# Hybrid decoder layer: first weight slice on ScalarE's queue in four pieces, its first cast and the bias table pinned in program order

## The chip, the cores and the metric

The kernel runs on one core of a Trainium2 chip. The metric is device time in microseconds (us), from the start of the program on the chip to its end; lower is better. The time before is the median of three runs.

## The reference

One layer of a hybrid decoder, one inference step over a prompt of 2048 rows and a sample batch of 8 rows, with D_MODEL = 1024:

```python
h = rmsnorm(x, g_norm)
proj = h @ w_in_l                       # 1024 x D_IN
(qa, ka, va, ga, ub, vb, gb, qc, kc, vc, gc, lr) = jnp.split(proj, offs, axis=-1)
ya = swa_prompt(qa, ka, va, rel_bias, sink_l)     # window 128, 8 heads of 64, 2 key heads
yb, v_rows = chunk_mlp(ub, vb, sw_l, sb_l, ln_g_l, ln_b_l)
oc, S_fin = gla(qc, kc, vc, log_a, s0)            # log_a from lr
...
y = jnp.concatenate([ya * jax.nn.silu(ga), yb * jax.nn.silu(gb), yc * jax.nn.silu(gc)], axis=-1)
x = x + (y @ w_out_l).astype(x.dtype)
```

Three mixers share one input projection: A is sliding-window attention with a learned sink for each head and a relative position bias taken from a table of 32 buckets, B a gated MLP over chunks of 128 rows, C a gated linear attention. An output projection and a final RMSNorm follow. Everything is float32.

## The kernel before, in words

**Tiling.** The prompt is cut into 16 x tiles of 128 rows (t = 0 to 15), and two of them make a chunk of 256 rows (c = 0 to 7). A float32 matmul is done as three float16 matmuls: each operand is split into a high and a low half, and PASSES (high by high, high by low, low by high) are summed in PSUM. The projection weights come in slices of columns: A1 holds the keys, the values and the low-rank gate (272 columns), A0 the queries (512), A2 the gate of A (512); the slices of B and C follow much later.

**An x tile.** `x_load` (L240) loads it from SyncE's queue into one of four buffers (`x_bufs`, named sl_1_105 for tiles 0, 1, 4, 5, ... and sl_2_106 for tiles 2, 3, 6, 7, ...). `h_tile` calls `norm_split`: ScalarE squares the tile with a running sum (L244), DVE works out the scale in a chain of small steps (L246, L124 to L134), ScalarE casts the scaled tile to the high half (L248), DVE takes the low half (L249). Then SyncE issues two DMA transposes (L258), one for each half, into a chunk buffer hb. TensorE needs these transposed tiles.

**A weight slice.** `prep_slice` returns five steps. `load` issues DMAs (L164) into float32 staging; for A1, which has two groups of columns, these are eight DMAs in before. `sq` squares it in four steps on ScalarE (L179). `sq2` sums the four columns over the partitions with one small matmul (L185) which is pinned by `tc.keep_in_program_order`, and DVE makes a scale from it (L187 to L192). `split(0, 4)` and `split(4, 8)` do eight casts on ScalarE (L203) and eight low halves on DVE (L204), one for each block of 128 rows of the slice.

**The units.** `unit_va` multiplies a tile by 144 columns of A1 (24 matmuls, L307) and is evicted by L456, L457 and L459; `unit_k` multiplies a chunk by the keys (24 matmuls, L296; evicted by L435 to L438); `unit_q`, four to a chunk, by the queries (L296; L476 on ScalarE, L477 on DVE); `unit_gate`, two to a chunk, by A2 (L307, 512 columns; L486 on ScalarE, L487 on DVE). TensorE works in the order: both tiles' `unit_va`, `unit_k` and four `unit_q` of the first chunk, the same of the second, their four gates, and then chunk by chunk.

**The bias table.** `lc_load` loads its inputs. `lc_bias` multiplies a one-hot table by the bias (L384), DVE copies the result (L386), SyncE writes it to DRAM (L387) and reads it back in two parts with overlapping windows (L391) into two buffers Lp. `lc_bm(0)` and `lc_bm(1)` reverse the rows with two float32 matmuls each (L398), which DVE scales into the table BM (L400). The first scores need BM.

**Attention of a tile.** For each tile and key head: `a_scores` (eight matmuls L506; DVE adds the bias and takes the maximum, L510), `a_soft` (L520 to L527), `a_exp` (L538, four exponentials), `a_split` (cast L548, low half on GpSimd L549, two DMA transposes L563), `a_pv` (L578, L583, L585), and the store of y (L588) after the second key head.

**What sets the order.** The program is traced once; `at(t, f)` puts a function on a list with a time, and `tick` counts the columns of the projection matmuls emitted so far as a clock and calls each function when its time has come. So the units' matmuls set the pace and the other work is traced between them. A scheduler then orders each engine's instructions by their dependences and its own costs; an instruction handed to `tc.keep_in_program_order` stays behind the one traced just before it on its engine. Each engine and each engine's DMA queue then runs strictly in its order. Before the first unit's matmuls, the code at L1300 to L1326 traces in order: `x_load(0)`, the small constants, `x_load(1)`, A1's load, a first part of A0's load, `h_tile(0)`, A1's `sq` and `sq2`, `h_tile(1)`, A1's two `split`s, the rest of A0's load, `x_load(2)`, `x_load(3)`, A2's load, the table's inputs, and A0's `sq`, `sq2` and `split`s. In the list stand `h_tile(2)` at 1, `lc_bias` at 2, `h_tile(3)` at 3, `lc_bm` at 7 and 9, A2's `sq` at 11, its `sq2` and first `split` at 14, its second `split` at 18.

Of the kernel before, what the change touches and what calls it, by code (L numbers as in the profile page):

```python
# [15 lines left out]
AF = mybir.ActivationFunctionType  # L16
# [17 lines left out]
OFF = {}  # L34
# [9 lines left out]
def hybrid_step_kernel(ctx: ExitStack, tc: tile.TileContext, I, O):  # L44
    nc = tc.nc
# [103 lines left out]

    def prep_slice(name, idx, cols, stage, dst, nload=1):  # L150
        n = sum(w for _, w in cols)
# [4 lines left out]
        def load_part(a, b):  # L156
            if "sg" not in st:
                st["sg"] = stage()
            for ap, k0, k1 in st["sg"]:
                lo, hi = max(a, k0), min(b, k1)  # L160
                c = 0
                for off, w in cols:
                    if lo < hi:
                        SP.dma_start(out=ap[:, lo - k0:hi - k0, c:c + w],  # L164
                                     in_=w_in[lo * 128:hi * 128, off:off + w].rearrange("(k p) n -> p k n", p=128))
                    c += w

        def load():
            for a in range(0, 8, 2):
                load_part(a, a + 2)  # L170

# [23 lines left out]
        def split(a, b):  # L195
            def f():
                for ap, k0, k1 in st["sg"]:
                    for k in range(max(a, k0), min(b, k1)):
# [3 lines left out]
                        gk = st["gs"][:, k:k + 1]  # L202
                        S.activation(out=hi, in_=src, func=AF.Copy, scale=gk)  # L203
                        V.scalar_tensor_tensor(out=lo, in0=src, scalar=gk, in1=hi, op0=ALU.mult, op1=ALU.subtract)  # L204
# [162 lines left out]
    lc = {}  # L367
# [26 lines left out]
    def lc_bm(half):  # L394
        def f():
            for q in range(2):
                ps = mbank()
                PE.matmul(ps, lc["fl"], lc[half][:, 2 * q:2 * q + 2, :].rearrange("p a b -> p (a b)"),  # L398
                          start=True, stop=True)
                V.tensor_scalar(out=BM["t"][:, half * 4 + 2 * q:half * 4 + 2 * q + 2, :].rearrange("p a b -> p (a b)"),  # L400
# [897 lines left out]

    if True:
        prA1 = prep_slice("A1", 0, [(OFF["ka"], 256), (OFF["lr"], 16)], stage_h(272), dst_one(272))  # L1300
        prA0 = prep_slice("A0", 1, [(OFF["qa"], 512)], stage_h(512), dst_slot(512))
        prA2 = prep_slice("A2", 2, [(OFF["ga"], 512)], stage_h(512), dst_slot(512))
        x_load(0)
        startup_consts()
        x_load(1)
        prA1[0]()
        LOADP["A0"][0]()
# [50 lines left out]
        at(3.0, lambda: h_tile(3))  # L1358
        at(7.0, lc_bm(0))
        at(9.0, lc_bm(1))  # L1360
        for t in range(4, NTILE):
# [163 lines left out]
```

## Time and profile before

| | before |
|---|---|
| median of three runs | 1192.56 us (1190.77 to 1195.80) |
| the profiled execution, its own time | 1196.03 us |
| its span in the trace | 1194.3 us |
| mean granted clock of TensorE | 0.99 |
| TensorE matmuls (PE) | 1136.0 us, 95% of the span |
| VectorE (DVE) | 677.2 us, 57% |
| ScalarE (ACT) | 480.9 us, 40% |
| GpSimd (POOL) | 72.9 us, 6% |

The times are device time of whole executions; the span is what the trace holds of the profiled one. PE is TensorE's matmuls, PEld its weight loads (which run beside matmuls), SPq a DMA's issue on SyncE. A busy share is an average over the whole span: what a stretch is worth is read from its waits and its timeline. In a row of a timeline the bracket gives how long the engine had been idle, and which instruction or DMA released it. [...]

### The profile page before, as it was taken

How to read it: one execution, taken by the hardware profiler on the slowest of the kernel's cores; microseconds unless marked ns; L12 is line 12 of the kernel's file. 1: busy time of each engine (PE TensorE's matmuls, PEld its weight loads, DVE VectorE, ACT ScalarE, POOL GpSimd, SP SyncE). 2: the span in 40 equal slices, each digit the busy share in tenths (PEclk: the TensorE clock that was granted, in tenths of full speed). 3: DMA queues.
4: the chain of work that ended last, by engine and by line, in shares of the span. 5: the costliest groups of instructions: out<-in, count | busy, mean ns of one | idle time of the engine just before them, and what ended most of it. 6: DMA issues, size and time to landing. Idle time of an engine off the chain costs nothing.

```text
span 1194.3 us, 19595 instructions
## 1 busy us (share of the span) xinstructions
PE 1136.0 (95%) x7637; PEld 663.4 (56%) x7637; DVE 677.2 (57%) x2229; ACT 480.9 (40%) x967; POOL 72.9 (6%) x49
## 2 busy tenths in 40 slices
PE   4997899997998999999999999999999999999997
PEld 3756577775654544444465567566665543444443
DVE  5887866657686355576284355645545643544442
ACT  7776755565771021552265411412212131322220
POOL 0012222222210000000000000000000000000000
PEclk9998999998999999999999999999999999999999
DMA  9579954534454002000054521220114446766641
GB/s 274 158 129 199 190 150 89 75 78 104 112 138 116 18 22 85 8 18 18 18 186 121 207 55 31 94 89 18 54 44 129 121 124 159 208 160 164 165 124 54
DMA packets 196913, 128.63 MB, mean 108 GB/s; under 512 B 155922, under 2 KB 170395, under 8 KB 196819
## 3 DMA queue, kind: packets, MB, share of 16 engines
q1 hardware_dynamic: 196818, 127.36, 41.4%
q8 instruction: 60, 0.98, 0.3%
q14 instruction: 35, 0.28, 0.1%
HBM read 66.36 MB, written 23.63 MB: 75 GB/s over the span
## 4 chain that ended last, share of the span: by engine, by line
PE 59%; DVE 3%; DMA 3%; ACT 2%; issue 1%; SPq 1%; POOL 0%; DVEq 0%; ACTq 0%
PE pp L307 31%; PE pp L1008 14%; PE pp L296 6%; DMA hb<-sl 2%; PE mx L671 1%; PE mx L867 1%; PE mx L849 1%; PE mx L873 1%; PE mx L881 1%; PE mx L320 1%; DMA sl<-y_d 1%; ACT sl L977 1%; SPq L989 1%; DVE sl L997 1%; DMA sl<-in_w_in_dram 0%
## 5 line engine op out<-in xcount | busy, mean ns | idle before, releaser
L307 PE MATMUL pp<-sl,hb 128*128 128x512 f16 x2304 | 516.9, 380 | 1.3 <-DVE qk L477 1.3
L307 PEld LDWEIGHTS <-hb 128*128 128x128 f16 x2688 | 250.2, 99 | 268.8 <-issue 12.5
L1008 PE MATMUL pp<-hb,hb 128*128 128x512 f16 x1152 | 251.2, 380 | 2.5 <-DMA hb<-sl 2.5
L1008 PEld LDWEIGHTS <-hb 128*128 128x128 f16 x1152 | 111.7, 98 | 140.3 <-DMA hb<-sl 5.4
L296 PE MATMUL pp<-hb,sl 128*128 128x256 f16 x1536 | 178.8, 275 | 8.7 <-DVE yy L487 8.6
L296 PEld LDWEIGHTS <-sl 128*128 128x128 f16 x1536 | 149.3, 98 | 31.9 <-issue 11.5
L549 POOL TENSOR_TENSOR phb<-Lp,pha 128x1024 f16<-128x1024 f32 (+1 forms) x32 | 66.5, 2079 | 288.0 <-ACT pha L548 270.9
L1011 DVE SCALAR_TENSOR_TENSOR sl<-pp,finv,sl 128x512 f32<-128x512 f32 x32 | 23.9, 748 | 85.8 <-PE pp L1008 85.8
L486 ACT ACTIVATE yy<-pp,scal 128x512 f32<-128x512 f32 x48 | 32.5, 679 | 81.5 <-PE pp L307 65.4
L994 ACT ACTIVATE sl<-sl 128x1024 f32<-128x1024 f32 (+1 forms) x16 | 16.9, 1056 | 116.8 <-DVE sl L1011 114.8
L538 ACT ACTIVATE Lp<-Lp,sm 128x256 f32<-128x256 f32 (+1 forms) x128 | 62.3, 488 | 0.2
L510 DVE CUSTOM_DVE_ANT_0 Lp<-mx,BM,scal 128x256 f32<-128x256 f32 (+1 forms) x128 | 54.7, 472 | 4.0 <-PE mx L506 3.4
L487 DVE SCALAR_TENSOR_TENSOR yy<-yy,pp 128x512 f32<-128x512 f32 x48 | 32.8, 682 | 42.2 <-ACT yy L486 42.2
L623 ACT ACTIVATE kk<-pp,invs 128x512 f32<-128x512 f32 x16 | 10.9, 683 | 93.3 <-PE pp L307 93.3
L477 DVE SCALAR_TENSOR_TENSOR qk<-pp,qk 64x256 f16<-64x256 f32 x64 | 26.9, 422 | 37.6 <-ACT qk L476 36.8
L978 DVE SCALAR_TENSOR_TENSOR sl<-sl,ch 128x1536 f16<-128x1536 f32 (+1 forms) x17 | 30.9, 1817 | 20.3 <-ACT sl L977 20.3
L977 ACT ACTIVATE sl<-sl,ch 128x1536 f16<-128x1536 f32 (+1 forms) x17 | 26.8, 1575 | 32.1 <-DVE ch L144 32.1
L637 DVE BATCH_NORM_STATS2 sm<-kk 128x6 f32<-128x512 f32 x16 | 11.1, 691 | 50.2 <-ACT kk L623 50.2
L204 DVE SCALAR_TENSOR_TENSOR sl<-sl,gs,sl 128x512 f16<-128x512 f32 x48 | 36.1, 813 | 3.6 <-ACT sl L203 3.3
L506 PE MATMUL mx<-kk,qk 128*128 128x256 f16 (+1 forms) x256 | 33.4, 271 | 4.7 <-DVE sm L510 4.7
L307 PE MATMUL pp<-s,hb 128*128 128x144 f16 x384 | 31.9, 246 | 5.9 <-DMA hb<-sl 3.6
L548 ACT CAST pha<-Lp 128x1024 f16<-128x1024 f32 (+1 forms) x32 | 32.4, 1012 | 5.1 <-DMA pt<-pha 4.7
(320 smaller groups left out, 1234.1 us busy)
## 6 DMA issues: line engine op xcount, KB each, us to landing
sl<-in_x_prompt_dram SPq DMA_DIRECT2D x32, 512.0 KB
sl<-in_w_in_dram SPq DMA_DIRECT2D x24, 512.0 KB
sl<-in_w_out_dram SPq DMA_DIRECT2D x6, 2048.0 KB
sl<-y_d SPq DMA_DIRECT2D x16, 768.0 KB
y_d<-yy SPq DMA_DIRECT2D x32, 256.0 KB
out_dram<-sl SPq DMA_DIRECT2D x15, 512.0 KB
hb<-in_w_in_dram SPq DMA_DIRECT2D x8, 512.0 KB
y_d<-Lp SPq DMA_DIRECT2D x8, 512.0 KB
```

What stands on the lines that cost most here:

```text
L204: V.scalar_tensor_tensor(out=lo, in0=src, scalar=gk, in1=hi, op0=ALU.mult, op1=ALU.subtract)
L296: PE.matmul(ps[:m, :CT], w[:, wl, k, c0:c0 + m], h[:, hl, k, :], start=(n == 0), stop=(n == 23))
L307: PE.matmul(ps[:, :n_], h[:, hl, k, j * 128:(j + 1) * 128], w[:, wl, k, c0:c0 + n_], start=(n == 0), stop=(n == 23))
L486: S.activation(out=g, in_=ps, func=AF.Tanh, scale=hg)
L487: V.scalar_tensor_tensor(out=g, in0=g, scalar=1.0, in1=ps, op0=ALU.add, op1=ALU.mult)
L506: PE.matmul(pv[:, hh, :], Qt[c][:, h // 2, h % 2, j * 128:(j + 1) * 128], Kt[c][:, 2 * hb + hl, ko:ko + W], start=(hl == 0), stop=(hl == 1))
L510: V.tensor_tensor_reduce(out=L[:, i, :], in0=pv[:, hh, :], in1=BM["t"][:, 4 * hb + i, 256 - W:256], scale=cS, scalar=-3e38, op0=ALU.add, o ...
L538: S.activation(out=L[:, i, :], in_=L[:, i, :], func=AF.Exp, bias=nb[:, i:i + 1], accum_out=den[:, i:i + 1])
L548: S.copy(P[0], L)
L549: G.tensor_tensor(out=P[1], in0=L, in1=P[0], op=ALU.subtract)
L977: S.activation(out=d["h"][:, 0, :], in_=d["y"], func=AF.Copy, scale=s)
L1008: PE.matmul(ps, d["yT"][:, hl, k, :], wo[k // 2][:, wl, k % 2, cs], start=(n == 0), stop=(n == 35))
```

## The change

Four things are edited.

- A1's load goes from SyncE's queue to ScalarE's, in two steps of four blocks in place of four steps of two. With A1's two groups of columns that makes four DMAs in place of eight; the bytes are the same. It is also traced ahead of the small constants and of `x_load(1)`.
- The first of A1's eight casts (k = 0) is pinned behind the ScalarE instruction traced just before it, which is x tile 1's cast in `h_tile(1)`.
- The four table matmuls (L398) are pinned in program order on TensorE.
- `lc_bm(0)` and `lc_bm(1)` are called at 12 and 14 in place of 7 and 9.

```diff
--- before.py
+++ after.py
@@ -147,7 +147,7 @@
     LOADP = {}
     INVI = {}
 
-    def prep_slice(name, idx, cols, stage, dst, nload=1):
+    def prep_slice(name, idx, cols, stage, dst, que=nc.sync, step=2):
         n = sum(w for _, w in cols)
         inv = invs[:, idx:idx + 1]
         INVI[name] = inv
@@ -161,13 +161,13 @@
                 c = 0
                 for off, w in cols:
                     if lo < hi:
-                        SP.dma_start(out=ap[:, lo - k0:hi - k0, c:c + w],
-                                     in_=w_in[lo * 128:hi * 128, off:off + w].rearrange("(k p) n -> p k n", p=128))
+                        que.dma_start(out=ap[:, lo - k0:hi - k0, c:c + w],
+                                      in_=w_in[lo * 128:hi * 128, off:off + w].rearrange("(k p) n -> p k n", p=128))
                     c += w
 
         def load():
-            for a in range(0, 8, 2):
-                load_part(a, a + 2)
+            for a in range(0, 8, step):
+                load_part(a, a + step)
 
         def sq():
             st["dst"] = dst()
@@ -200,7 +200,9 @@
                         hi = st["dst"][:, 0, k, :]
                         lo = st["dst"][:, 1, k, :]
                         gk = st["gs"][:, k:k + 1]
-                        S.activation(out=hi, in_=src, func=AF.Copy, scale=gk)
+                        cast = S.activation(out=hi, in_=src, func=AF.Copy, scale=gk)
+                        if name == "A1" and k == 0:
+                            tc.keep_in_program_order(cast)
                         V.scalar_tensor_tensor(out=lo, in0=src, scalar=gk, in1=hi, op0=ALU.mult, op1=ALU.subtract)
             return f
 
@@ -395,8 +397,8 @@
         def f():
             for q in range(2):
                 ps = mbank()
-                PE.matmul(ps, lc["fl"], lc[half][:, 2 * q:2 * q + 2, :].rearrange("p a b -> p (a b)"),
-                          start=True, stop=True)
+                tc.keep_in_program_order(PE.matmul(ps, lc["fl"], lc[half][:, 2 * q:2 * q + 2, :].rearrange("p a b -> p (a b)"),
+                                                   start=True, stop=True))
                 V.tensor_scalar(out=BM["t"][:, half * 4 + 2 * q:half * 4 + 2 * q + 2, :].rearrange("p a b -> p (a b)"),
                                 in0=ps, scalar1=rS, scalar2=-3e38, op0=ALU.mult, op1=ALU.max)
         return f
@@ -1297,13 +1299,14 @@
         return out
 
     if True:
-        prA1 = prep_slice("A1", 0, [(OFF["ka"], 256), (OFF["lr"], 16)], stage_h(272), dst_one(272))
+        prA1 = prep_slice("A1", 0, [(OFF["ka"], 256), (OFF["lr"], 16)], stage_h(272), dst_one(272),
+                          que=nc.scalar, step=4)
         prA0 = prep_slice("A0", 1, [(OFF["qa"], 512)], stage_h(512), dst_slot(512))
         prA2 = prep_slice("A2", 2, [(OFF["ga"], 512)], stage_h(512), dst_slot(512))
         x_load(0)
+        prA1[0]()
         startup_consts()
         x_load(1)
-        prA1[0]()
         LOADP["A0"][0]()
         h_tile(0)
         prA1[1]()
@@ -1356,8 +1359,8 @@
         at(1.0, lambda: h_tile(2))
         at(2.0, lc_bias)
         at(3.0, lambda: h_tile(3))
-        at(7.0, lc_bm(0))
-        at(9.0, lc_bm(1))
+        at(12.0, lc_bm(0))
+        at(14.0, lc_bm(1))
         for t in range(4, NTILE):
             at(HT0 + HTD * (t - 4) - HTL, lambda t=t: x_load(t))
             at(HT0 + HTD * (t - 4), lambda t=t: h_tile(t))
```

The change moves instructions on several queues. Lines of the changed kernel are 2 higher than before from L206 on, and 3 higher from L1304 on; buffer numbers differ.

**ScalarE at the start.** hb_126 and hb_127 (before) or hb_108 and hb_109 (after) are the two halves of A1's staging; sl_105 is x tile 0 and then 1; ch_140 and ch_174 (ch_136 and ch_170) are the scales of x tile 0 and 1; hb_136 (hb_132, hb_133) is A0's staging. Before:

```order
L244 ACTIVATE sl_105,ch_140<-sl_105 128x1024
L179 ACTIVATE s_14_156,sm_157<-hb_126 128x544
L248 ACTIVATE sl_105<-sl_105,ch_140 128x1024
L179 ACTIVATE s_14_156,sm_157<-hb_126 128x544
L179 ACTIVATE s_14_156,sm_157<-hb_127 128x544 x2
L244 ACTIVATE sl_105,ch_174<-sl_105 128x1024
L203 ACTIVATE s_14_156<-hb_126,gs_172 128x272 x4
L203 ACTIVATE s_14_156<-hb_127,gs_172 128x272 x4
L248 ACTIVATE sl_105<-sl_105,ch_174 128x1024
L179 ACTIVATE sl_227,sm_228<-hb_136 128x1024 x2
```

After, where four DMA issues of A1 (L164) also stand ahead of these rows:

```order
L246 ACTIVATE sl_105,ch_136<-sl_105 128x1024
L179 ACTIVATE s_14_152,sm_153<-hb_108 128x544 x2
L179 ACTIVATE s_14_152,sm_153<-hb_109 128x544
L250 ACTIVATE sl_105<-sl_105,ch_136 128x1024
L179 ACTIVATE s_14_152,sm_153<-hb_109 128x544
L179 ACTIVATE sl_223,sm_224<-hb_132 128x1024
L246 ACTIVATE sl_105,ch_170<-sl_105 128x1024
L203 ACTIVATE s_14_152<-hb_108,gs_168 128x272 x3
L203 ACTIVATE s_14_152<-hb_109,gs_168 128x272 x4
L179 ACTIVATE sl_223,sm_224<-hb_132 128x1024
L250 ACTIVATE sl_105<-sl_105,ch_170 128x1024
L203 ACTIVATE s_14_152<-hb_108,gs_168 128x272
```

The cast that is pinned stands behind x tile 1's cast, by itself, and the seven others ahead of it; an A0 square and x tile 1's square now stand ahead of the casts, and a second A0 square ahead of x tile 1's cast.

**TensorE at the table's matmuls.** Lp is the table read back, sm_225 (sm_221) the reversing matrix. Before, they stand behind all of the first chunk's units and 23 matmuls of the second chunk's first `unit_va` (pp_555), with A2's sum L185 behind them:

```order
L307 LDWEIGHTS hb_282
L307 MATMUL pp_555<-s_14_156,hb_282 128x144
L398 MATMUL mx_415<-Lp_328,sm_225 128x512
L398 MATMUL mx_418<-Lp_328,sm_225 128x512
L398 MATMUL mx_448<-Lp_330,sm_225 128x512
L398 MATMUL mx_451<-Lp_330,sm_225 128x512
L185 MATMUL mx_515<-sm_478,ones 128x4
L307 LDWEIGHTS hb_282
L307 MATMUL pp_555<-s_14_156,hb_282 128x144
```

After, the first two stand ahead of the last matmul of the first chunk's third `unit_q` (pp_454); the other two come ten matmuls later, in the fourth (pp_495), with A2's sum behind them:

```order
L298 MATMUL pp_454<-hb_135,sl_223 128x256
L298 LDWEIGHTS sl_223
L298 MATMUL pp_454<-hb_135,sl_223 128x256
L400 MATMUL mx_476<-Lp_324,sm_221 128x512
L400 MATMUL mx_479<-Lp_324,sm_221 128x512
L298 LDWEIGHTS sl_223
L298 MATMUL pp_454<-hb_135,sl_223 128x256
L298 LDWEIGHTS sl_223
L298 MATMUL pp_495<-hb_135,sl_223 128x256
```

So the table's matmuls moved ahead by most of a `unit_q` and the 23 matmuls of `unit_va`, although their times in the list are later. A0's sum (L185) moved as well: it stood behind 26 projection matmuls and stands behind 8 now.

**SyncE's queue when chunks 3 and 4 are loaded and transposed.** With numbers: pt is a transposed probability (L563), hb_386 chunk 3's buffer, hb_458 chunk 4's. Before:

```order
L563 DMA_TRANSPOSE pt_983<-pha_973 128x8x128
L563 DMA_TRANSPOSE pt_983<-phb_974 128x8x128
L258 DMA_TRANSPOSE hb_1077<-sl_106 128x8x128 x4
L258 DMA_TRANSPOSE hb_1585<-sl_105 128x8x128 x2
L240 DMA sl_106<-in_x_prompt_dram 128x1024
L563 DMA_TRANSPOSE pt_1074<-pha_1065 128x8x128
L563 DMA_TRANSPOSE pt_1074<-phb_1066 128x8x128
L588 DMA y_d<-yy_1002 128x512
L240 DMA sl_106<-in_x_prompt_dram 128x1024
L240 DMA sl_105<-in_x_prompt_dram 128x1024
```

After:

```order
L260 DMA_TRANSPOSE hb_1073<-sl_106 128x8x128 x2
L242 DMA sl_106<-in_x_prompt_dram 128x1024
L260 DMA_TRANSPOSE hb_1073<-sl_106 128x8x128
L565 DMA_TRANSPOSE pt_979<-pha_969 128x8x128
L565 DMA_TRANSPOSE pt_979<-phb_970 128x8x128
L260 DMA_TRANSPOSE hb_1073<-sl_106 128x8x128
L260 DMA_TRANSPOSE hb_1581<-sl_105 128x8x128 x2
L242 DMA sl_106<-in_x_prompt_dram 128x1024
L242 DMA sl_105<-in_x_prompt_dram 128x1024
L565 DMA_TRANSPOSE pt_1070<-pha_1061 128x8x128
L565 DMA_TRANSPOSE pt_1070<-phb_1062 128x8x128
L590 DMA y_d<-yy_998 128x512
```

The loads of x into sl_2_106 and sl_1_105 that stood behind the transposes into pt_385 and the store of y stand ahead of both now, and two of the four transposes into hb_386 stand ahead of those into pt_367. Earlier in this queue a transpose of x tile 2 stands between the table's write and the first of its two reads, where before a transpose and an x load stood there.

## Rows read from the trace of the kernel before

**Rows 1.** The page, part 1: busy time, share of the span and instructions of each engine.
```profile
PE 1136.0 (95%) x7637; PEld 663.4 (56%) x7637; DVE 677.2 (57%) x2229; ACT 480.9 (40%) x967; POOL 72.9 (6%) x49
```

**Rows 2.** Waits of TensorE, whole span: who waited, for whom; total us, times, longest.
```profile
PE mx L506 <- DVE sm L510: 4.7, 4, 2.7
...
PE pp L307 <- DVE qk L477: 1.3, 1, 1.3
```

**Rows 3.** Windows: us, busy (count) of five engines, granted clock, DMA share, GB/s.
```profile
0.00:10.00 10.00, 1.17 (x4) 0.61 (x4) 2.30 (x13) 4.11 (x6) 1.50 (x10) 1.00 0.83 223
...
16.00:18.00 2.00, 1.95 (x14) 1.31 (x13) 2.00 (x9) 1.59 (x5) 0.00 (x0) 1.00 1.05 406
...
44.00:46.00 2.00, 1.15 (x2) 0.64 (x3) 0.00 (x0) 0.00 (x0) 0.00 (x0) 0.59 1.18 348
...
90.00:120.00 30.00, 22.47 (x245) 18.68 (x244) 22.71 (x98) 18.07 (x42) 6.38 (x3) 0.89 1.02 196
```

**Rows 4.** Timeline of ScalarE, start: start us, us, instruction, idle before it and releaser.
```profile
4.83 1.06 ACT L244 ACTIVATE sl<-sl 128x1024 bf16<-128x1024 f32 x1 [2.82 <-DMA sl<-in_x_prompt_dram]
...
11.29 0.64 ACT L179 ACTIVATE s<-hb 128x544 bf16<-128x544 f32 x1
...
14.04 3.41 ACT L203 ACTIVATE s<-hb,gs 128x272 f16<-128x272 f32 x8 [0.98 <-DVE ch L246]
...
17.86 1.15 ACT L248 ACTIVATE sl<-sl,ch 128x1024 f16<-128x1024 f32 x1 [0.41 <-DVE ch L134]
...
25.19 5.01 ACT L203 ACTIVATE sl<-hb,gs 128x512 f16<-128x512 f32 x8 [0.83 <-DVE gs L192]
```

**Rows 5.** Timeline of SyncE's queue and TensorE, 19 to 34 us.
```profile
19.03 2.67 SPq L258 DMA_TRANSPOSE hb<-sl  x2
...
22.65 0.42 PE L307 MATMUL pp<-s,hb 128*128 128x144 f16 x2 [3.62 <-DMA hb<-sl]
...
23.83 2.85 PE L307 MATMUL pp<-s,hb 128*128 128x144 f16 x22
...
29.38 4.97 PE L296 MATMUL pp<-hb,sl 128*128 128x256 f16 x44
```

**Rows 6.** Timeline of TensorE and SyncE's queue around the bias table, 34 to 51 us.
```profile
34.27 0.81 PE L384 MATMUL mx<-yy,relx 33*8 33x384 f32 x2
...
35.01 5.85 PE L296 MATMUL pp<-hb,sl 128*128 128x256 f16 x52
...
39.65 0.93 SPq L391 DMA_DIRECT2D Lp<-e_d  x2
...
40.70 1.60 PE L307 MATMUL pp<-s,hb 128*128 128x144 f16 x23
...
44.85 5.12 PE L398 MATMUL mx<-Lp,sm 128*128 128x512 f32 x8 [2.55 <-DMA Lp<-e_d]
...
48.52 0.19 PEld L398 LDWEIGHTS mx<-Lp,sm 128*128 128x128 f32 x1 [0.24 <-issue]
...
48.95 0.19 PEld L398 LDWEIGHTS mx<-Lp,sm 128*128 128x128 f32 x1 [0.24 <-issue]
...
50.01 0.61 PE L506 MATMUL mx<-kk,qk 128*128 128x128 f16 x8
```

**Rows 7.** Timeline of ScalarE, A2's casts.
```profile
53.66 2.55 ACT L203 ACTIVATE sl<-hb,gs 128x512 f16<-128x512 f32 x4
```

**Rows 8.** Timeline around the longest gap, 93 to 108 us, all engines.
```profile
93.93 1.26 SPq L563 DMA_TRANSPOSE pt<-pha  x1
...
97.35 1.28 DVE L249 SCALAR_TENSOR_TENSOR sl<-sl,ch 128x1024 f16<-128x1024 f32 x1 [1.33 <-ACT sl L248]
...
98.00 1.79 SPq L240 DMA_DIRECT2D sl<-in_x_prompt_dram  x2
...
99.50 0.60 PE L506 MATMUL mx<-kk,qk 128*128 128x256 f16 x4 [1.21 <-DVE sm L510]
...
107.43 0.80 PE L296 MATMUL pp<-hb,sl 128*128 128x256 f16 x3 [6.02 <-DVE yy L487]
```

## The prediction, on record before the changed kernel ran

> **What bounds the kernel now.** First I read the engine totals: TensorE is busy for 1136.0 us of the 1194.3 us span [rows 1]. So only its idle gaps and the stretches at half clock can be won. Next come TensorE's waits [rows 2]: 4.7 us in four waits for the score evictions of L510 (longest 2.7), 1.3 us for L477 in one. The timelines of the first 110 us then show the long ones. At 22.65 TensorE has waited 3.62 us for the transposed second tile [rows 5]; at 44.85 it has waited 2.55 us for the bias table [rows 6]; at 107.43 it has waited 6.02 us for L487 [rows 8]. [...] The table's eight half matmuls take 5.12 us, while the last ones among them start 0.43 us apart (48.52, 48.95) [rows 6]: at that pace eight take 3.4. TensorE's own order changes only ahead of the first score matmul; the other queues' orders differ up to the eighth chunk's tiles or so, and are the same from there on. So I price the first 110 us and carry it to the end.
>
> **The change, part by part.** Times are on the clock of the profiled execution; lines are those of before. The mark to compare is the first score matmul, at 50.01 [rows 6]: behind it TensorE's order is unchanged.
>
> *A1's load from ScalarE.* Four DMA issues go ahead of ScalarE's table load. ScalarE waits 2.82 us for x tile 0 at 4.83 [rows 4]; an issue costs 0.47 us by SyncE's rows (98.00: 1.79 for two, 0.9 at the most) [rows 8]. So 1.9 us are covered by 2.82; at 0.9 each it would put 0.8 us on the path. I take nothing. SyncE is spared eight issues, but the pieces were not waiting for the issue alone: up to 10 us the DMA engines are 0.83 busy at 223 GB/s [rows 3]. That is 2.23 MB, and A1 (1.11 MB) with x tiles 0 and 1 (1.05 MB) are 2.16 MB. A1's last piece had landed by 11.29, when its fourth square starts [rows 4]. In the changed order the same bytes stand ahead of it, on two queues. By bytes alone it is there at 9.7; if the two first A0 pieces get in between (0.52 MB at 406 GB/s [rows 3], 1.3 us each), at 13.2. I take 10.6, near the row of before. [...]
>
> *ScalarE's order.* Once A1 has landed, ScalarE does: third A1 square 0.64, x0's cast 1.15, fourth square and read-out 0.8 (13.2; before about 12), one A0 square and x1's square at 1.06 each (15.5; the scale, 2 us behind the fourth square as before, is ready), seven A1 casts at 3.41/8 = 0.43 (18.5), another A0 square (19.6), x1's cast 1.15 (20.7; before 19.01), the held cast 0.43 (21.1), two A0 squares (23.3) [rows 4]. So x1's two transposes are asked for 1.7 us later than 19.03. Before, the second of them let TensorE go on 3.5 us after its issue (19.03 plus half of 2.67, to 23.83) [rows 5]. So 25.5 now.
>
> *TensorE up to the table.* It does 8 matmuls of the first unit, is held by A0's sum (L185) until 23.9, and then does the other 16 at 2.85/22 = 0.13 us (26.0), the second tile's 24 (29.1), unit_k's 24 at 0.113 from the row at 35.01, 5.85/52 [rows 6] (31.8; before 29.38 [rows 5]). So the new start of the first slice costs 2.4 us and saves none: the 3.62 us gap is filled with the work that used to stand ahead of it, and the second tile is later. A0's casts start at 25.4, behind an A2 square and x2's square, against 25.19 [rows 4], and hold nobody up.
>
> *The table.* L384 runs 0.8 us after 11 matmuls of unit_q (33.0 to 33.8), DVE copies by 34.4, the write goes out at 34.5. In SyncE's order a transpose of x tile 2 then stands ahead of the first table read, and it waits for a ScalarE cast that I place at 35.3 (A0's casts to 30.4, then two small casts, x3's square, two key casts, an A2 square, the cast itself 1.15). So the read goes out at 36.6. Before, reads issued at 39.65 let TensorE go at 44.85, 5.2 us [rows 6], with an x load and a transpose ahead of them. With the transpose alone I get 40.0 (transpose issue plus 3.5, plus 1.3 for 0.52 MB); with 5.2 it is 41.8. TensorE is due there at 31.8 + 2.7 + 0.8 + 2.7 + 2.6 = 40.6. I take that: no wait. Then 2 x 0.85 (two halves each), ten matmuls 1.1, 2 x 0.85, L185 0.3, fifteen matmuls 1.7, 24 short ones at 1.60/23 = 0.07 (1.7) [rows 6]: 48.8, against 50.01. **Term 1: -1.2** (2.4 lost at the start, 2.55 of wait and 1.7 of half clock won; the other 0.6 is the first tile's work that now lies inside).
>
> *A2's casts.* In before they start at 53.66 and hold ScalarE for 5 us [rows 7] just where the second chunk's casts are due; TensorE's 1.3 us for L477 [rows 2] come from that. A2's sum stands behind the table still, so it comes at 45.1 in place of 49.8, so they start about 6 us earlier. **Term 2: -1.3.**
>
> *The 6.02 us gap.* It ends when the gate eviction has passed, and that stood on ScalarE behind the squares of x tiles 11 and 12, whose loads SyncE issued at 98.00, behind two transposes and a y store that took it from 93.93 [rows 8]. Now these loads are ahead of that work, by 4 us and more. The squares then no longer wait for a DMA; but three exponentials now stand ahead of that eviction. Working forward from the scores at 99.50: I estimate the maxima at 101.5, two us behind the scores, 1.2 for the exponentials and 1.5 for the gate's two evictions (L486, L487): 104.2 in place of 107.43. **Term 3: -3.2.** Also, x tile 9's cast stands ahead of the fourth softmax now, so DVE's 1.28 us at 97.35 [rows 8] are out of the way of the scores, and the 1.2 us wait before 99.50 (one of four in the 4.7 of rows 2) goes. **Term 4: -1.2.**
>
> The sum is -6.9. The profiled execution took 1196.03 us, which gives 1189.1; it lies 3.5 us above the median of the runs, 1192.56. On the median: **1185.7 us**.
>
> Bounds. Term 1: 0 to -1.8 as the table lands (41.8, 40.0) and A1 does (9.7); +1.4 if A1 comes at 13.2, +1.7 more if the wait for the table is long enough to bring the clock down again. Term 2: 0 to -1.3. Term 3: 0 to -6.0, and -2.6 more if the half clock behind it goes too. Term 4: 0 to -1.2. A new wait of the kind of the 6.02 us one is possible for every transpose that moved.
>
> **Rivals.** *Start gain only.* From 90 to 120 us the DMA engines are at 1.02 [rows 3]: the transposes fill them. If the queue is what is short, moving x loads forward only makes the probability transposes late, and TensorE waits for those. Then term 1 alone stays: 1191.4. For it speaks the full share, against it that some of the moved transposes now go ahead of the stretch, to where the queue asks for less.
>
> *Slower: two queues share the engines.* With A1's small pieces (64-byte rows) beside the 2 KB rows of A0, A1's last piece comes at 13.2, not 10.6. ScalarE's queue is in order, and x0's cast, x1's cast, A0's squares and x2's cast all stand behind it: 2.6 us later. The mark is at 51.4 (+1.4), the table is late as well, with the clock down (+1.7) and 1.3 more for the longer read: +4.4, and nothing is won behind it: 1197.0. It decides once A1 lands after about 12. For it speaks that the engines are nearly full already [rows 3]; against it that SyncE must wait for x0 and A1 pieces before it asks for more. [...]
>
> *All of it goes.* With tiles transposed earlier every DMA wait up to 150 us is gone: terms 2 and 4, 6.0 and 2.6 of half clock at the gap, 1.2 at the start, and 1.5 of the 2.7 us wait for L510 [rows 2]: -13.8, or 1178.8.
>
> **How the numbers follow.** Chances: forecast 0.48 (1182 to 1189), start only 0.22, slower 0.17, all of it 0.13. About 0.5% (6 us, below 1186.6 or above 1198.5) is what a measurement of this kernel tells from no change. The forecast lies just beyond that: 0.28 of its 0.48, with 0.12 of the last case, make 0.40 for faster. Of the slower rival 0.07 is beyond 6 us. The rest, 0.53, is no difference. The range is from 1178, below the last case, to 1197, the slower rival.
>
> **What would show it.** Right: TensorE's first short matmuls at 21 us or later, no gap of 3.6 us before 24 us, the table matmuls at 40 to 42 us with a granted clock of 1.00, the first score matmul at 48 to 49.5, A2's casts before 49, and a gap below 3 us near 103. Wrong, if the third A1 square starts after 12, if the clock falls below 1.00 before 50 us, or if a wait of several us for a transposed tile stands between 70 and 110.

## The result, and the profile after

The changed kernel took 1201.62 us (median of 6 runs, 1200.22 to 1203.50), the kernel before in the same job 1193.84 (6 runs, 1190.77 to 1196.61). The ratio is 1.0067 with a 95% interval of 1.0046 to 1.0088: 7.8 us slower, where 1185.7 was forecast. The profiled execution of the changed kernel took 1203.50 us; its span is 1201.7. TensorE's busy time is the same, 1135.6 us beside 1136.0 [rows 1]; only its idle time grew.

The page of the changed kernel, part 1:

```profile
PE 1135.6 (94%) x7637; PEld 662.8 (55%) x7637; DVE 681.1 (57%) x2229; ACT 481.9 (40%) x967; POOL 72.4 (6%) x49
```

TensorE's waits in the changed kernel (who waited, for whom: total us, times, longest). Lines are 2 higher than before.

```profile
PE pp L298 <- DVE yy L489: 9.8, 4, 4.1
...
PE pp L309 <- ACT s L203: 6.9, 1, 6.9
PE mx L185 <- ACT s L179: 6.6, 1, 6.6
PE mx L508 <- DVE sm L512: 5.7, 4, 2.2
```

In the kernel before:

```profile
PE pp L296 <- DVE yy L487: 8.6, 3, 6.0
...
PE mx L185 <- ACT s L179: 3.0, 1, 3.0
```

Two waits grew: 6.6 us for A1's squares (ahead of A1's sum), where 3.0 stood, and 6.9 us for A1's held cast, where the first unit waited 1.95 for a cast. The wait for the table shrank from 2.55 to 1.7 [rows 6]. The gate's evictions (L489) cost 9.8 us in four waits, longest 4.1, in place of 8.6 in three, longest 6.02 [rows 8]; the score evictions 5.7 in place of 4.7 [rows 2].

ScalarE at the start of the changed kernel (start us, us, instruction, idle before it and what ended that):

```profile
7.75 0.64 ACT L179 ACTIVATE s<-hb 128x544 bf16<-128x544 f32 x1
...
15.36 0.66 ACT L179 ACTIVATE s<-hb 128x544 bf16<-128x544 f32 x1 [6.88 <-DMA hb<-in_w_in_dram]
...
17.05 0.64 ACT L179 ACTIVATE s<-hb 128x544 bf16<-128x544 f32 x1
...
19.80 2.99 ACT L203 ACTIVATE s<-hb,gs 128x272 f16<-128x272 f32 x7
```

Two of A1's squares are done by 8.4, and then ScalarE stands idle for 6.88 us, because the second half of A1 is not there. The fourth square starts at 17.05 in place of 11.29 [rows 4], the casts at 19.80 in place of 14.04 [rows 4], the held cast ends at 25.3.

TensorE in the changed kernel, from its first projection matmul:

```profile
25.33 0.28 PE L309 MATMUL pp<-s,hb 128*128 128x144 f16 x1 [6.91 <-ACT s L203]
...
30.94 2.82 PE L309 MATMUL pp<-s,hb 128*128 128x144 f16 x22 [0.49 <-DMA hb<-sl]
33.55 3.98 PE L298 MATMUL pp<-hb,s 128*128 128x256 f16 x24
...
47.81 1.98 PE L400 MATMUL mx<-Lp,sm 128*128 128x512 f32 x4 [1.68 <-DMA Lp<-e_d]
...
56.04 0.61 PE L508 MATMUL mx<-kk,qk 128*128 128x128 f16 x8
...
72.41 5.99 PE L309 MATMUL pp<-sl,hb 128*128 128x512 f16 x27
...
101.31 1.47 PE L298 MATMUL pp<-hb,s 128*128 128x256 f16 x12 [0.78 <-DVE yy L489]
...
103.85 0.60 PE L508 MATMUL mx<-kk,qk 128*128 128x256 f16 x4 [0.63 <-DVE sm L512]
...
109.83 0.49 PE L298 MATMUL pp<-hb,sl 128*128 128x256 f16 x3 [4.08 <-DVE yy L489]
...
120.61 0.60 PE L508 MATMUL mx<-kk,qk 128*128 128x256 f16 x4 [2.25 <-DVE sm L512]
...
155.59 0.80 PE L298 MATMUL pp<-hb,sl 128*128 128x256 f16 x3 [3.70 <-DVE yy L489]
```

The same matmuls of the kernel before that are not among the rows ahead of the prediction:

```profile
68.07 1.25 PE L307 MATMUL pp<-sl,hb 128*128 128x512 f16 x5 [1.31 <-DVE qk L477]
...
116.16 1.04 PE L506 MATMUL mx<-kk,qk 128*128 128x256 f16 x8
...
149.12 0.49 PE L296 MATMUL pp<-hb,sl 128*128 128x256 f16 x3 [1.38 <-DVE yy L487]
```

Laid side by side, the first score matmul (the mark of the prediction) is 6.03 us late (56.04 against 50.01 [rows 6]). At the first gate matmul the kernel has won 1.7 of that back (72.41 against 68.07: 4.34), at the end of the long gap 3.6 (109.83 against 107.43 [rows 8]: 2.40). Then it loses again: the second half of the scores that start at 116.16 before and had no wait inside them now waits 2.25, and the matmuls of 149.12 start 6.47 late. At the end it is 7.4.

It is not carried evenly from there to the end. The same matmuls are 7.5 us late at 182.05 (174.55 before), 2.8 at 297.53 (294.72 before), 3.4 at 368.89 (365.49) and 7.5 at 377.90 (370.42). In these two executions the first step is a wait of the kernel before, the second one of the changed kernel:

```profile
286.75 1.88 PE L334 MATMUL mx<-selg,yy 128*128 128x8 f32 x8 [3.44 <-ACT yy L329]
...
372.04 1.09 PE L611 MATMUL mx<-ident,phb 128*128 128x128 f32 x4 [2.50 <-DMA phb<-in_spatial_w_dram]
```

In the other kernel these waits are 0.75 and 0.91 us. Beside the longer wait the granted clock, a share of TensorE's full speed, is 0.57 (286 to 294 us before, 370 to 378 in the changed kernel), and 1.00 in the same stretch of work of the other kernel (292 to 300, 366 to 372). So the start is 6.0 us of the loss, and what the prediction hoped to win behind the mark was won and given back; that the end stands so near the mark is in part chance, two steps of about 4 us that cancel.

### The profile page after: what moved, and what is told of

Read it like the earlier page. It is cut to its first block, busy times and chain, and to the rows that moved or that the text cites. A ratio compares the mean times of both kernels' runs of the same rounds, so it can differ in the third digit from the quotient of the medians.

```text
span 1201.7 us, 19596 instructions
## 1 busy us (share of the span) xinstructions
PE 1135.6 (94%) x7637; PEld 662.8 (55%) x7637; DVE 681.1 (57%) x2229; ACT 481.9 (40%) x967; POOL 72.4 (6%) x49
## 3 DMA queue, kind: packets, MB, share of 16 engines
q10 hardware_dynamic: 2112, 1.11, 0.3%
## 4 chain that ended last, share of the span: by engine, by line
PE 59%; DVE 3%; DMA 3%; ACT 2%; issue 1%; SPq 1%; POOL 0%; DVEq 0%; ACTq 0%
PE pp L309 31%; PE pp L1010 14%; PE pp L298 6%; DMA hb<-sl 1%; PE mx L869 1%; PE mx L673 1%; PE mx L851 1%; PE mx L875 1%; PE mx L883 1%; PE mx L322 1%; DMA sl<-y_d 1%; ACT sl L979 1%; SPq L991 1%; DVE sl L999 1%; PE mx L345 0%
## 5 line engine op out<-in xcount | busy, mean ns | idle before, releaser
L489 DVE SCALAR_TENSOR_TENSOR yy<-yy,pp 128x512 f32<-128x512 f32 x48 | 32.7, 682 | 42.2 <-ACT yy L488 42.2
L309 PE MATMUL pp<-s,hb 128*128 128x144 f16 x384 | 29.2, 238 | 8.5 <-ACT s L203 6.9
L206 DVE SCALAR_TENSOR_TENSOR sl<-sl,gs,sl 128x512 f16<-128x512 f32 x48 | 35.1, 794 | 2.2 <-ACT sl L203 2.2
```

The costliest lines, as they stand in the source:

```text
L309: PE.matmul(ps[:, :n_], h[:, hl, k, j * 128:(j + 1) * 128], w[:, wl, k, c0:c0 + n_], start=(n == 0), stop=(n == 23))
L489: V.scalar_tensor_tensor(out=g, in0=g, scalar=1.0, in1=ps, op0=ALU.add, op1=ALU.mult)
```

## The experiments

Theory Q was: A1's last piece lands late because it shares the DMA engines with SyncE's queue, and that costs the time. Its rival P: the pins do, the held cast above all. All times below are medians beside runs of the kernel before on the same chip. The code cuts show the lines that matter, and their comments are not in the kernels but say what else belongs to the edit; line numbers shift by a few from kernel to kernel.

**load_only**: the new queue, no pins, table at 7 and 9. In the kernel before:

```diff
-        x_load(0)
-        startup_consts()
-        x_load(1)
-        prA1[0]()
+        x_load(0)
+        prA1[0]()                # que=nc.scalar, step=4
+        startup_consts()
+        x_load(1)
```

> Kernel before with A1's load alone changed: four pieces on ScalarE's queue, asked for ahead of the constants; no pins, table times 7 and 9. Theory Q (shared engines): on the second queue A1's last DMA, the 16-column piece, moves one descriptor for one of SyncE's big ones and lands late, and this alone makes the change slower: the fourth A1 square starts after 14.5 us (11.29 before), the first score matmul comes at 53.5 to 57 (50.01 before, 56.04 with the whole change), and the time is 4 to 9 us above before. Theory P (pins): the held cast and the table's pin cost the time; then this kernel is within 3 us of before, with the fourth square before 12.5.

Measured: 1203.77 against 1194.08, ratio 1.0082 (1.0061 to 1.0103). ScalarE and TensorE of this kernel:

```profile
15.42 0.66 ACT L179 ACTIVATE s<-hb 128x544 bf16<-128x544 f32 x1 [7.10 <-DMA hb<-in_w_in_dram]
...
57.70 0.61 PE L506 MATMUL mx<-kk,qk 128*128 128x128 f16 x8
```

The load alone makes the whole loss and 2 us more: theory Q, with the mark 0.7 us and the time 0.7 us beyond what it expected.

**cast_only**: the pin on the k = 0 cast alone, in the kernel before.

```diff
-                        S.activation(out=hi, in_=src, func=AF.Copy, scale=gk)
+                        cast = S.activation(out=hi, in_=src, func=AF.Copy, scale=gk)
+                        if name == "A1" and k == 0:
+                            tc.keep_in_program_order(cast)
```

> Kernel before with the k = 0 cast of A1 pinned behind x tile 1's cast, nothing else. Theory Q: the first unit starts at 18.5 to 19.5 in place of 14.61, but the second tile's transposes are asked for 0.4 us earlier and they decide, so the second tile starts at 23 to 24 (23.83 before), the first score matmul is within 2 us of 50.0 unless the reordered queue moves the table, and the time is within 3 us of before. Theory P: the first unit's lost work is not made up, the second tile starts at 26 or later, and the time is 4 us or more above before.

Measured: 1194.67 against 1194.08, ratio 1.0011 (0.9997 to 1.0025). TensorE:

```profile
19.51 0.28 PE L309 MATMUL pp<-s,hb 128*128 128x144 f16 x1 [6.79 <-ACT s L203]
...
50.24 0.61 PE L508 MATMUL mx<-kk,qk 128*128 128x128 f16 x8
```

The first unit starts 4.9 us later and costs nothing by the mark: it fills the gap of 3.62 us that stood ahead of the second tile, which follows at 24.04 (23.83 before) and does its 22 matmuls in 1.54 us in place of 2.85. As the main cause, P falls.

**table_only**: the table's matmuls pinned and called at 12 and 14, in the kernel before.

```diff
-                PE.matmul(ps, lc["fl"], ...
+                tc.keep_in_program_order(PE.matmul(ps, lc["fl"], ...
...
-        at(7.0, lc_bm(0))
-        at(9.0, lc_bm(1))
+        at(12.0, lc_bm(0))
+        at(14.0, lc_bm(1))
```

> Kernel before with the four table matmuls pinned and called at 12 and 14, nothing else; TensorE's order of them stays behind 23 matmuls of the second chunk's first unit. Theory Q: same as before within 2 us, with the wait for the table 2 to 3 us at about 44.9. Theory P in its table form: slower by 3 us or more.

Measured: 1194.53 against 1194.08, ratio 1.0005 (0.9991 to 1.0019), with a wait of 2.18 us for the table at 45.07: no difference, as theory Q has it.

**load_undone**: the changed kernel with the load as before.

```diff
-        x_load(0)
-        prA1[0]()                # que=nc.scalar, step=4
-        startup_consts()
-        x_load(1)
+        x_load(0)
+        startup_consts()
+        x_load(1)
+        prA1[0]()                # que=nc.sync, step=2
```

> The changed kernel with A1's load put back on SyncE's queue in eight pieces, both pins and the later table kept. Theory Q: the fourth A1 square starts at 11.3 as before, and the time is within 3 us of before, 5 us or more under the changed kernel. Theory P: it stays within 2 us of the changed kernel, about 1201.

Measured: 1196.10 against 1194.08, ratio 1.0026 (1.0008 to 1.0045), where the changed kernel has 1.0067: some 5 us of the loss went with the load, a little less than the 5.5 that the medians of the two jobs give. The two pins together cost 2 us, by an interval that leaves out zero; neither alone can be told from nothing.

The next three ask how the two queues share. The profile names a packet count for each queue: q1 is SyncE's, q10 ScalarE's. In the changed kernel, between 11 and 13 us (packets, MB, share of the 16 engines' time):

```profile
q1 hardware_dynamic: 271, 0.73, 99.7%
q10 hardware_dynamic: 243, 0.02, 9.8%
```

Nearly as many packets of each queue went by, with 0.73 MB on SyncE's and 0.02 on ScalarE's. The trace has the size of each packet, and it is that of a row: of the 243 on ScalarE's queue 236 hold 64 bytes, the row of the 16-column piece; of the 271 on SyncE's 155 hold 2 KB, the row of A0, and 100 hold 4 KB, the row of x tiles 2 and 3. That led to theory A: the queues take turns by packet. The turns are not equal in every stretch (399 to 518 from 8 to 11 us), but nearly so in sum: up to 14.7 us, when ScalarE's queue has passed the last of its packets, it is 2149 to 2112. Worked out from the shapes, A1's four pieces are 4 x 512 = 2048 rows; SyncE's x tiles 0 to 3, the norm column (1024 elements, in packets of 4 bytes) and two A0 pieces come to 4 x 128 + 1024 + 2 x 256 = 2048 as well.

**lr_first**: the changed kernel with ScalarE's own DMAs in another order.

```diff
-            for a in range(0, 8, step):
-                load_part(a, a + step)
+            for only in ([16, 256] if name == "A1" else [None]):
+                for a in range(0, 8, step):
+                    load_part(a, a + step, only)     # only pieces of this width
```

> The changed kernel with ScalarE's four DMAs in another order, both 16-column pieces ahead of both 256-column ones; every other queue and engine keeps its order. Theory A (the queues take turns by descriptor, so what counts is how many descriptors stand in ScalarE's queue): the number is the same, so A1 is complete no earlier than 14 us and the third A1 square or the fourth starts at 14 or later (15.36 for the third in the changed kernel); time within 3 us of 1201.6. Theory B (the queues share bytes, and only a piece of 64-byte rows at the end is slow): the last piece of big rows lands at 11 to 12, the squares are done by 13, the first score matmul comes 2.5 us or more earlier than 56.04 and the time is 1196 to 1199.

Measured: 1202.80 against 1193.81, ratio 1.0069 (1.0041 to 1.0096). Its queues between 11 and 13 us:

```profile
q1 hardware_dynamic: 186, 0.62, 80.8%
q10 hardware_dynamic: 178, 0.18, 26.4%
```

ScalarE and TensorE:

```profile
15.79 0.66 ACT L180 ACTIVATE s<-hb 128x544 bf16<-128x544 f32 x1 [3.71 <-DMA hb<-in_w_in_dram]
...
32.90 2.78 PE L299 MATMUL pp<-hb,s 128*128 128x256 f16 x24
...
53.92 0.61 PE L509 MATMUL mx<-kk,qk 128*128 128x128 f16 x8
```

With the small rows gone first, big rows of 1 KB stand at the end, and the half still arrives at 15.8. Again packet for packet, 186 to 178. So it isn't that a piece of small rows is slow, and not a share by bytes (0.62 MB to 0.18): what counts here is how many packets stand in the queue, 2112 in the changed kernel. Theory A. The mark is 2.1 us earlier than in the changed kernel all the same, for another reason (last section).

**lr_on_sync**: the changed kernel, the two 16-column pieces on SyncE's queue.

```diff
-                        que.dma_start(out=ap[:, lo - k0:hi - k0, c:c + w],
+                        (que if w > 16 else nc.sync).dma_start(out=ap[:, lo - k0:hi - k0, c:c + w],
```

> The changed kernel with the two 16-column pieces of A1 issued by SyncE right behind x tile 0; ScalarE's queue keeps the two 256-column pieces. Theory A: half the descriptors are left in ScalarE's queue, so A1 is complete at 10 to 11.5, near the 11.06 at which its third piece of the changed kernel was in; the fourth square starts at about 11, the first score matmul comes at 50 to 52.5, and the time is 1191 to 1197. If instead a second queue by itself is what costs: fourth square at 13.5 or later, and the time stays at 1199 to 1203.

Measured: 1192.18 against 1193.81, ratio 0.9989 (0.9974 to 1.0004): the loss of 7.8 us is gone with two DMAs of 32 KB. ScalarE and TensorE:

```profile
8.79 0.64 ACT L179 ACTIVATE s<-hb 128x544 bf16<-128x544 f32 x1
...
47.85 0.61 PE L508 MATMUL mx<-kk,qk 128*128 128x128 f16 x8
...
106.37 0.80 PE L298 MATMUL pp<-hb,sl 128*128 128x256 f16 x3 [6.62 <-DVE yy L489]
```

The third square, which waited until 15.36, starts at 8.79 with no wait; the fourth, expected at about 11, starts at 12.04, behind x tile 0's cast. The mark, expected at 50 to 52.5, is 2.2 us earlier than in the kernel before, and 0.95 earlier than the 48.8 that I forecast. The gap at 107 is still there.

**x_held**: the changed kernel, x tiles 2 and 3 held behind A0's pieces.

```diff
-        SP.dma_start(out=xt, in_=xp[t * 128:(t + 1) * 128, :])
+        ld = SP.dma_start(out=xt, in_=xp[t * 128:(t + 1) * 128, :])
+        if t in (2, 3):
+            tc.keep_in_program_order(ld)
```

> The changed kernel with the loads of x tiles 2 and 3 held behind A0's four pieces on SyncE's queue, where they stood in the kernel before. Theory A: the last 16-column piece has big descriptors of SyncE's opposite it only as long as A0's second piece lasts, so it lands at 12.5 to 13.3 in place of 15.3; the third A1 square at about 13, the first score matmul 1 to 2.5 us earlier than 56.04, and the time 1198 to 1200.5. If the competitor does not matter (the piece is slow by itself): the third square at 15 or later, time 1200 to 1203.

Measured: 1205.91 against 1193.81, ratio 1.0102 (1.0078 to 1.0126). ScalarE and TensorE:

```profile
13.18 0.66 ACT L179 ACTIVATE s<-hb 128x544 bf16<-128x544 f32 x1 [4.77 <-DMA relx<-in_rel_bias_dram]
...
52.49 0.61 PE L510 MATMUL mx<-kk,qk 128*128 128x128 f16 x8
```

Half right. The start is as theory A has it (13.18, and the mark 3.5 us earlier; the releaser's name is that of a small load which landed at the same time). From 3 to 11 us the queues pass 1655 and 1853 packets; from 11 to 13 it is 764 on SyncE's, then full of small rows, to 259 on ScalarE's, which is empty before 13. The time is a miss: 5 us more than expected. The x tiles that come later move the whole of SyncE's order; the 3.5 us won at the mark and 3.2 more (its span is 1204.9) were lost behind it, and where was not taken apart.

**no_cast_pin**: the changed kernel without the pin on the cast.

```diff
-                        if name == "A1" and k == 0:
-                            tc.keep_in_program_order(cast)
```

> The changed kernel without the pin on the k = 0 cast. The first unit starts at about 20.5 in place of 25.33, and is held by A1's other work; x tile 1's cast stands 0.4 us later, so its transposes are asked for 0.4 us later. If the second tile decides: it starts at 30.5 to 33.5, the first score matmul within 2.5 us of 56.04, the time 1200 to 1205, near load_only (1203.8). If the held cast was a loss of its own: 1197 to 1199.

Measured: 1205.16 against 1194.48, ratio 1.0085 (1.0071 to 1.0099). The second tile's main run of TensorE starts at 33.27, the mark is 56.57:

```profile
33.27 2.82 PE L307 MATMUL pp<-s,hb 128*128 128x144 f16 x22 [2.11 <-DMA hb<-sl]
...
56.57 0.61 PE L506 MATMUL mx<-kk,qk 128*128 128x128 f16 x8
```

As the expectation for the case in which the second tile decides, but for a time at its upper end. The held cast was no loss; whether it was a gain beside the late load (1.0067 with, 1.0085 without, intervals that overlap) stays open.

**lr_sync_no_pins**: load_only with the two small pieces on SyncE's queue (the edit of lr_on_sync).

> load_only with the two 16-column pieces issued by SyncE behind x tile 0: the new queue without either pin and with the table's times 7 and 9. It asks whether turns by packet explain the whole loss of load_only (9.7 us above before). If they do: A1 complete at 8 to 9, the first unit at about 15.5, the second tile at 25 to 26.5, the first score matmul at 47 to 49.5, and the time within 3 us of before. If the new order of SyncE's and ScalarE's work costs by itself: 1197 or more.

Measured: 1194.44 against 1194.48, ratio 1.0002 (0.9992 to 1.0012). Its mark is at 49.05, as expected. Of the 9.7 us of load_only nothing is left. That settles the main cause. With A1 in time the pins cost nothing either (lr_on_sync, which has them: 0.9989).

**lr_sync_gcol**: lr_on_sync with the norm column's load ahead of the small pieces.

```diff
         x_load(0)
-        prA1[0]()
         startup_consts()
+        prA1[0]()
         x_load(1)
```

> The kernel lr_on_sync with the norm column's load (1024 elements of 4 bytes) ahead of the two 16-column pieces on SyncE's queue, not behind them. In lr_on_sync that column kept TensorE's first small matmul waiting until 9.19 us, and A1's sum until 12.82. If the queues take turns by packet, the column lands before 6.5, A1's sum comes at 10.5 to 12, x tile 1's cast up to 1.2 us earlier than 18.83, the first score matmul at 46.5 to 47.8 (47.85 there, 50.01 before), and the time is 1189.5 to 1193, 1 to 4 us under before. Rival: A0's square, which stands ahead of x tile 1's square and waits for A0's first piece (11.4), holds ScalarE anyway; then the mark stays at 47.5 to 48 and the time at that of lr_on_sync, 1192.

Measured: 1193.85 against 1194.48, ratio 0.9990 (0.9981 to 0.9999). TensorE:

```profile
9.00 0.58 PE L360 MATMUL mx<-ident,sm 128*1 128x128 f32 x2 [9.00 <-DVE ch L248]
...
47.70 0.61 PE L508 MATMUL mx<-kk,qk 128*128 128x128 f16 x8
...
105.96 0.80 PE L298 MATMUL pp<-hb,sl 128*128 128x256 f16 x3 [6.42 <-DVE yy L489]
```

The mark and the time are the rival's, but not its reason: the column arrives hardly earlier (9.00 against 9.19 for the matmul that needs it). Theory A, used properly, says so, by an estimate from the shapes: the column's 1024 packets stand opposite the 1024 rows of 1 KB that are all of ScalarE's queue there. This is the only kernel here whose interval against the kernel before lies below 1, and only just; by 0.1%, one of thirteen compared, no gain is shown.

**all_casts**: the kernel before with all eight A1 casts pinned behind x tile 1's (cast_only's edit without `and k == 0`).

> The kernel before with all eight casts of A1 pinned behind x tile 1's cast, load and table as before. It asks what the held cast would be worth if the whole group moved: x tile 1's cast no longer waits for 3.41 us of casts. The second tile's transposes are asked for 2 to 3 us earlier than 19.03, the first unit starts at 16.5 to 18 in place of 14.61, the second tile at 20.5 to 22 in place of 23.83. Theory Q (what decides is when the second tile comes): TensorE gains 2 us at the start, the table and A0's casts give part of it back, and the time is 1 to 4 us under before. Rival: A0's casts, which start at 25 either way, set the pace, the gain is gone by 35 us, and the time is within 1.5 us of before.

Measured: 1198.25 against 1193.81, ratio 1.0038 (1.0025 to 1.0050). TensorE and ScalarE:

```profile
22.12 2.33 PE L309 MATMUL pp<-s,hb 128*128 128x144 f16 x24
...
27.45 3.16 ACT L203 ACTIVATE sl<-hb,gs 128x512 f16<-128x512 f32 x5
...
49.78 0.61 PE L508 MATMUL mx<-kk,qk 128*128 128x128 f16 x8
```

Both expectations missed. The second tile came earlier (22.12), A0's casts later (27.45 against 25.19 [rows 4]), so the start was even; and 4.4 us were lost behind it. The waits for the gate's evictions grew from 8.6 to 12.5 us (longest 6.7); what made them longer wasn't tried.

**gcol_later_x**: lr_sync_gcol, the casts and transposes (`h_tile`) of the x tiles from the fifth on called two units later. Their loads are called at HT0 less HTL, which stays 4; so, other than the expectation says, the loads keep their times and stand earlier against the transposes.

```diff
-    HT0, HTD, HTL = 22, 11, 18
+    HT0, HTD, HTL = 24, 11, 20
```

> lr_sync_gcol with the loads and transposes of x tiles from the fifth on asked for 2 units of the list later (24 in place of 22). Its start is the same (first score matmul at 47.7). In its SyncE order chunk 4's transposes stand behind the transposes of the probabilities pt_385 and the store of y, as in the kernel before, but both loads into sl_106 stand ahead of them. If the 6 us gap comes from x loads issued late, it falls under 3 us and the time is 1188 to 1192. If the probabilities' transposes are what is short on that queue, the gap or a wait of the same size comes back within 30 us, and the time is 1192 to 1197.

Measured: 1197.85 against 1195.77, ratio 1.0021 (1.0010 to 1.0033). TensorE:

```profile
96.26 2.72 PE L298 MATMUL pp<-hb,s 128*128 128x256 f16 x12 [4.83 <-DVE yy L489]
...
105.33 0.80 PE L298 MATMUL pp<-hb,sl 128*128 128x256 f16 x3 [3.29 <-DVE yy L489]
```

The gap of 6.42 became two, of 4.83 and 3.29: 8.1 us together. Loads that are asked for earlier in SyncE's queue moved the gap and did not shorten it. The time came in at 1197.85, just above the 1192 to 1197 of the case in which the probabilities' transposes are short.

## Why the prediction was wrong

**The step that failed is "I take 10.6"**, the time at which A1's last piece is there. It was the first of the sum, and both its bounds, 9.7 and 13.2, were worked out by bytes. The piece came at 15.3 (the third square starts at 15.36), outside the bounds. The queues shared by packets: 243 to 271 in 2 us. From 9.4 to 14.7 us, in which the last piece of 32 KB came in, SyncE's queue moved 1.79 MB. The rival "two queues share the engines" had the mechanism and its point (third square after 12), with a chance of 0.17, and by the same mistake gave 13.2 and 1197.0. The row for the share of the engines [rows 3] was read by bytes, "the same bytes stand ahead of it, on two queues"; the shapes in the code, 64 bytes a row beside 2 KB a row, were named in the rival and not counted.

Up to 14.7 us the two queues passed 2149 and 2112 packets, SyncE's with 3.13 MB and ScalarE's with 1.11: it was turns that came out nearly even, and not bytes. Why the queues take turns, and what sets the uneven ones, no run here shows.

**What ScalarE did with it** was right in kind and size. I had its casts at 15.5 after a fourth square that ends at 13.2; the square ended at 17.7 and the casts began at 19.80, 4.3 later against 4.5. The transposes of x tile 1 then took 4.01 us to issue and not 2.67 [rows 5], and the second tile's matmuls ran from 30.94, where I had them follow the first tile's at 26.0. SyncE's queue:

```profile
24.89 4.01 SPq L260 DMA_TRANSPOSE hb<-sl  x2
```

That this tile decides and not the first unit is shown by no_cast_pin: the first unit starts at 20.41 there, 4.9 us earlier than in the changed kernel, TensorE then waits 2.06 and 2.11 us for the second tile, and the mark is no earlier (56.57).

**Term 1** (-1.2) was therefore +6.0. With A1 in time (lr_on_sync) the mark came at 47.85, 0.95 ahead of the 48.8. That is near, but in part by luck: the keys were done at 30.0 and not 31.8, and the table's matmuls stand later in that kernel's order and came at 42.57 after a wait of 1.20, where I had 40.6 and none. Of the 1.7 us of half clock in this term 1.4 were won there: the eight half matmuls took 3.70 us behind that wait, 5.12 behind 2.55 in the kernel before, 5.40 behind 2.18 in table_only. That the wait brings the clock down was my estimate; no run changes the wait alone.

**Term 2** (-1.3): the wait for L477 is gone, and the kernel is 1.7 nearer at 72.41. As forecast in size, though A2's casts start at 55.28 and not before 49; in the changed kernel they are 1.6 us later than in before, while the mark is 6.0 later.

**Terms 3 and 4** (-4.4) named the right places and took the wait for the loads as the price. The waits there fell from 6.02 and 1.21 to 4.08, 0.78 and 0.63: 1.7 us. But 2.25 and 3.70 stand at 120.61 and 155.59, where 0 and 1.38 stood; over the whole span the two kinds of wait add up to 15.5 us, and to 13.3 before. And the clock was down at the first (118 to 125 us):

```profile
118.00:125.00 7.00, 4.75 (x47) 3.84 (x45) 6.79 (x28) 4.81 (x13) 0.67 (x1) 0.76 1.09 186
```

In the kernel before the same window reads 1.00. SyncE's and ScalarE's queues of the changed kernel there:

```profile
101.77 6.76 SPq L260 DMA_TRANSPOSE hb<-sl  x4
...
109.74 1.23 SPq L565 DMA_TRANSPOSE pt<-pha  x1
...
115.42 1.04 ACT L550 CAST pha<-Lp 128x1024 f16<-128x1024 f32 x1 [4.17 <-DMA pt<-pha]
```

Four transposes of x stand ahead of a probability transpose, which goes out at 109.74 (105.42 before, behind two); the cast that needs its buffer waits 4.17 us at 115.42, and an x tile's cast, two squares and the key evictions stand behind it on ScalarE, and the score evictions on DVE behind the low half of that x tile. That is the rival "start gain only", in its words "moving x loads forward only makes the probability transposes late". The trace shows this chain; gcol_later_x, in which the gap came back as two, speaks for it; no run took that wait away by itself, so its price is argued and not shown.

**Carried to the end.** The prediction priced the first 110 us and took the sum to the end. The two steps near 290 and 370 us, each of about 4 us, show that the rest of the span does not pass a lateness on unchanged. They cancel here; nothing in the prediction made them do so.

## What to carry to other kernels

Before a load goes to a second DMA queue, count its rows and those that the other queue holds at the same time. In the counts of this case the two queues took turns and did not share the bytes (243 packets with 0.02 MB beside 271 with 0.73): a piece of few bytes in many short rows waited for about one long row of the other queue for each of its own. What helped here was to leave the long rows that are urgent on the second queue and to put the short ones on the first (lr_on_sync, 0.9989 in place of 1.0067). And read a gain at a gap that a queue sets by asking what the same queue then does later: here the gap of 6.02 us shrank (4.08 in the changed kernel), stayed (6.62 in lr_on_sync) or split (4.83 and 3.29 in gcol_later_x) with each order of the queue, and none that was tried removed it.

## What the runs showed that I had not expected

Two DMAs of 32 KB on ScalarE's queue decided 9.7 us (load_only against lr_sync_no_pins, 1203.77 and 1194.44, each beside 1194). The same bytes on SyncE's queue cost nothing that can be measured (1.0002, 0.9992 to 1.0012).

In the changed kernel 24 matmuls of `unit_k` took 3.98 us at 33.55, and in lr_first, with the same order of matmuls, 2.78 at 32.90, with no wait in either row. Both profiles print a granted clock of 1.00 there. TensorE's windows of the changed kernel (us, busy time and count, granted clock, DMA share, GB/s):

```profile
34.00:36.00 2.00, 2.00 (x11) 1.00 1.00 252
36.00:38.00 2.00, 2.00 (x20) 1.00 0.91 266
```

The pace nearly doubles at 36 us, from 11 matmuls in 2 us to 20, whatever the column says. The first clock record in the trace stands at that point: at 36.0 us in the changed kernel, 27.3 in the kernel before; ahead of it the 1.00 has no record behind it. In lr_first the pace rose at 32.0 by estimate: its second tile's 22 matmuls from 31.09 took 1.97 us, where all of them at the slow pace took 2.82 (the changed kernel) and all at the fast one 1.54 (cast_only). With the second tile's 22 matmuls (2.82 us against 1.97) the earlier rise is worth 2.1 us to lr_first, about all that its mark is ahead. Of the 6.0 us at the changed kernel's mark some 0.7 are of this kind by estimate, as the kernel before takes 3.07 us for 23 of the same matmuls, at 26.47. Why the pace rose 4 us earlier in lr_first, with A1 no earlier, stays open.
